# A hybrid encoder layer on one Trainium2 core: reordering the gate chain, delaying weight casts, pairing the gate projection, summing a chunk in PSUM

## Chip, core and metric

One NeuronCore of a Trainium2 chip runs the whole layer in one launch. The metric is the device time of that launch in microseconds (us); the kernel is timed in several runs, and the median is given. A further execution was recorded by the hardware profiler; its time stands beside its span below. Engines: TensorE (PE, with its weight loads PEld), VectorE (DVE), ScalarE (ACT), GpSimd (POOL), and SyncE (SP), which issues most DMAs.

## The reference, cut to what matters

An input x of 2048 positions x 1024 channels, float32, goes through one projection, two token mixers and an output projection:

```python
proj = einsum('bsd,de->bse', x, w_in[l])
q, k, v, gf_lr, gb_lr, z_gla, u, z_fnet = split(proj, _OFFSETS)
log_af = log_sigmoid(einsum(gf_lr, w_gate_up_fwd) + b_gate_fwd) / 16    # and log_ab for the other direction
o = gla_chunked(q * dk**-0.5, k, v, log_af) + flip(gla_chunked(flip(q), ..., flip(log_ab)))
o = o * rsqrt(mean(o * o, -1) + RMS_EPS)                                # per head
y_gla = o * gla_norm_g * silu(z_gla)
y_fnet = (real(fft2(u)) @ w_fnet) * silu(z_fnet)
y = concat([y_gla, y_fnet]) @ w_out
x = layernorm(alpha * x + y, ln_g, ln_b)
```

gla_chunked is gated linear attention (S_t = diag(a_t) S_{t-1} + k_t^T v_t, o_t = q_t S_t): inside a chunk, masked and decay-scaled scores times v; between chunks, a carried state S.

## The kernel before

Positions are cut into 8 blocks of 256 (`BLK`), each of two chunks of 128. Float32 operands are split into a high part in a reduced format (a ScalarE cast, line 55) and a low part (a VectorE subtraction, line 58); a product is three matmuls (high x high, high x low, low x high). `self.split` is the helper for both, so casts of x, of weights and of `mix` all carry lines 55 and 58. A scheduler of the language orders each engine's instructions at compile time, by the order of the source and by when it believes each to be ready. `tc.issue_after(ins)` adds an edge: every instruction in its block that runs on the engine of `ins` comes behind `ins` on that engine; instructions on other engines are not touched. Semaphores follow from the data.

PSUM has eight banks under three names: four `mm`, two `pa`, two `pg`.

*Phase 1* starts with the gate projection z_gla (`zg_first`, then `zg_block`). `zg_first` does blocks 0 and 1 while the weights arrive. `zg_block` does one block: for each of 4 column groups c, `proj_t` (line 86) runs 24 matmuls of 256 columns into one bank, and `zg_out` evicts it with Silu (262), scales it (263) and stores it (264). `load_x` brings the next block of x in two halves of 512 KB, a block ahead. A generator `bg` prepares the weights of the next stage in between. The other two projections, u and z_fnet, follow (line 349). `consts` casts the gate weights (466).

*Phase 2* is the Fourier mixer beside the q and k projections.

*Phase 3* (lines 898 to 953) loops over the blocks. For block b, in the order of the source: `pw_part` and `pv_part` (line 94) project v and the gate ranks; `gate_evac` and `gate_t` (755 to 788) turn the ranks (`rn`, `R`); `gates` (790) multiplies by the gate weights (798), applies Abs, Exp and Ln on ScalarE (800 to 803), finishes the log-sigmoid on VectorE (804) and runs two scans (809, 811): the first half of the gate chain. `gates2` (817), called an iteration later for the same block, is the second half: four small ScalarE copies (821 to 824), a VectorE subtraction and clip (825, 826), two ScalarE exponentials (828, 829), the scaling of q and k on VectorE (`scaled`, 845 and 846) and the decay factors (`alphas`). Then, for each chunk, `gla_a`: scores of both directions (855, 856), a transpose of the keys (859), the mask on VectorE (861, 862, tile `at`) and the eviction of the transposed keys on ScalarE (864, tile `ks`). `gla_b`: the state increment (874) from `ks`, evicted into S (876, 878), and the inner output (881) from `at`, evicted into `oi` (882). `gla_a` of a block's second chunk stands at the end of an iteration, its `gla_b` in the next. `chain_f` carries the forward state on GpSimd (`chain_step`, 1089 and 1092).

In iterations 2 to 5 `wof_load` brings half of the output weights: it loads two pieces of 256 KB (988) and splits them (989) in the same call. Behind the loop come `gates2` of block 7, `p4_start` (loads, `mix` heads and the other output weights), the first half of the output product of chunks 15 and 14 (`outp`, 1113) and the last two chunks' attention.

*Phase 4* goes over the chunks from 15 down. `prep(n)` carries the backward state (1149), multiplies q by the state (1153), adds `oi` (1155), squares (1157) and splits; `norm(n)` normalises, gates and splits into `mix`; `outp` adds the attention half to the output product; `finish` does the layer norm.

Each engine works through its own queue in order; SyncE's queue holds nearly all DMAs.

Of the kernel before, what the change touches and what calls it, by code (L numbers as in the profile page):

```python
# [19 lines left out]
P = 128  # L20
# [23 lines left out]
class Kern:  # L44
# [94 lines left out]
    def phase1(self):  # L139
# [3 lines left out]
        with ExitStack() as ctx:  # L143
# [116 lines left out]
            def zg_out(b, c, ps, zp):  # L260
                zs = zp.tile([P, BLK], F32, name="zs", tag=f"t{c}")
                nc.scalar.activation(out=zs, in_=ps, func=AF.Silu)
                nc.scalar.activation(out=zs, in_=zs, func=AF.Copy, scale=self.gn[:, c:c + 1])
                nc.sync.dma_start(out=self.zg_d[b][:, c], in_=zs)

            def zg_block(b, xh, bg, zp):
                for c in range(4):
                    ps = self.mm([P, BLK])
                    self.proj_t(ps, xh, self.wzg, c * P)
                    zg_out(b, c, ps, zp)  # L270
                    next(bg, None)

            with ExitStack() as rctx:
# [3 lines left out]
                xn = self.load_x(2)  # L277
# [4 lines left out]
                for b in range(2, NBLK - 1):  # L282
                    xh, xn = xn, self.load_x(b + 1)
                    zg_block(b, xh, bg, rp)
# [81 lines left out]
            def run(u, c, p, x):  # L366
# [56 lines left out]
            zg_block(NBLK - 1, xn, nxt, st)  # L423
# [28 lines left out]
    def consts(self):  # L452
# [13 lines left out]
        nc.scalar.copy(out=wg[0:97], in_=wgr)  # L466
# [258 lines left out]
    def phase3(self):  # L725
# [16 lines left out]
        with ExitStack() as ctx:  # L742
# [47 lines left out]
            def gates(b, blk):  # L790
                R = blk["R"]
                pool = gp if b % 2 else ga
                g = pool.tile([P, 4, BLK], F32, name="g", tag="g")
                for i in range(2):
# [6 lines left out]
                    with self.tc.issue_after(self.preload.ins):  # L801
                        nc.scalar.activation(out=gi, in_=gi, func=AF.Exp, scale=-1.0)
                    nc.scalar.activation(out=gi, in_=gi, func=AF.Ln, bias=one, scale=1.0)
# [40 lines left out]
            def scaled(blk):  # L844
                V.tensor_tensor(out=blk["q"], in0=blk["q"], in1=blk["eq"], op=ALU.mult)
                V.tensor_tensor(out=blk["ek"], in0=blk["kr"], in1=blk["ek"], op=ALU.mult)
                blk["k"] = blk["ek"]

            def gla_a(b, t, blk):
# [12 lines left out]
                V.copy_predicated(at.rearrange("p h i -> p (h i)"), mb, ab.rearrange("p h i -> p (h i)"))  # L862
                ks = gp.tile([P, 4, P], F32, name="ks", tag="ks", bufs=2)
                nc.scalar.copy(out=ks, in_=kt)  # L864
                blk["ak"].append((at, ks))

            def gla_b(b, t, blk):
# [12 lines left out]
                for h in range(4):  # L880
                    nc.tensor.matmul(op[:, h * P:(h + 1) * P], v[:, h * P:(h + 1) * P], at[:, h], start=True, stop=True)  # L881
                nc.scalar.copy(out=blk["oi"][:, t], in_=op)
# [14 lines left out]

            wof = self.wof_load()
            prev, old, xn = None, None, self.load_x(0)
            for b in range(NBLK):  # L900
# [9 lines left out]
                if b > 1:  # L910
                    gates2(b - 1, prev)
# [19 lines left out]
                if b == 1:  # L931
                    with self.tc.issue_after(R_ev.ins):
                        gates2(0, prev)
                elif b > 1:
# [18 lines left out]
            self.find_range(gp)  # L953

# [27 lines left out]
    def wof_load(self):  # L982
        nc = self.nc
        w = self.wof = self.wpool.tile([P, 2, 4, 1024], F32R, name="wB_w", tag="wB")
        for k in range(4):
            for c in range(0, 1024, 512):
# [289 lines left out]
```

## Time and profile before

| | us |
|---|---|
| median of 3 runs | 812.93 |
| lowest, highest | 809.15, 814.84 |
| profiled execution: its time | 808.7 |
| its span, first to last instruction | 806.8 |
| TensorE busy in the span | 758.7 |
| VectorE busy | 549.5 |
| ScalarE busy | 384.9 |
| GpSimd busy | 190.0 |

A busy time says how long an engine had an instruction running; it doesn't say whether the engine sets the time. That is read from its waits: for each instruction that started late, the profile names what released it.

### The profile page before, as it was taken

The page shows a single profiled execution, that of the slowest core. Times are in us where ns is not written, and L with a number is a line of the kernel's source. Part 1 is how long each engine was busy: PE and PEld are TensorE (multiplying, and loading weights), DVE is VectorE, ACT ScalarE, POOL GpSimd, SP SyncE. Part 2 cuts the span into 40 slices and gives each one's busy share as a digit, 9 for nine tenths or more (in the row PEclk, how much of TensorE's full clock was granted, in tenths as well). Part 3 has the DMA queues.
Part 4 walks back from the last instruction along what each step waited for, and adds up shares of the span by engine and source line. Part 5 has one row for each costly group of instructions (what it writes and reads, how often), then busy time and mean ns, then how long its engine had stood idle before and what let it go on. Part 6 is the DMA issues. An engine that isn't in the chain of part 4 may idle for free.

```text
span 806.8 us, 14100 instructions
## 1 busy us (share of the span) xinstructions
PE 758.7 (94%) x5542; PEld 713.7 (88%) x5542; DVE 549.5 (68%) x802; ACT 384.9 (48%) x730; POOL 190.0 (24%) x139
## 2 busy tenths in 40 slices
PE   7999999999999998999998898888798999999995
PEld 6999999999999998999997798887786788888884
DVE  4692197454535899776568887777667876776764
ACT  6684453322223534435346776756645344344341
POOL 0000003020201000321400421233234644644431
PEclk9999999999999999999999999998999999999998
DMA  8864434514136782647764655634247445435321
GB/s 253 255 223 157 149 110 143 165 66 144 66 113 185 242 284 89 191 143 223 229 183 157 184 175 191 183 107 132 76 137 281 146 159 189 157 138 178 107 89 70
DMA packets 76609, 130.52 MB, mean 162 GB/s; under 512 B 7315, under 2 KB 48787, under 8 KB 76534
## 3 DMA queue, kind: packets, MB, share of 16 engines
q1 hardware_dynamic: 74230, 125.34, 48.4%
q10 hardware_dynamic: 2304, 4.20, 1.5%
q8 instruction: 45, 0.74, 0.4%
q14 instruction: 30, 0.25, 0.1%
HBM read 92.81 MB, written 36.70 MB: 161 GB/s over the span
## 4 chain that ended last, share of the span: by engine, by line
PE 67%; DVE 17%; DMA 6%; ACT 5%; issue 3%; SPq 1%; POOL 0%; DVEq 0%; ACTq 0%; POOLq 0%
PE mm L1113 19%; PE mm L349 19%; PE mm L86 13%; PE mm L94 5%; DVE c L811 2%; DVE c L809 2%; PE pa L609 2%; DMA fw<-u_d 2%; PE pa L1153 2%; DVE g L825 1%; DVE fw L508 1%; PE pg L874 1%; DVE fw L505 1%; PE mm L231 1%; PE pg L881 1%
## 5 line engine op out<-in xcount | busy, mean ns | idle before, releaser
L94 PE MATMUL mm<-wA_w,xhl 128*128 128x272 f32 x768 | 106.2, 294 | 0.0
L94 PEld LDWEIGHTS mm<-wA_w,xhl 128*128 128x128 f32 x768 | 100.0, 192 | 0.0
L86 PE MATMUL mm<-xhl,wC_w 128*128 128x256 f32 x768 | 96.0, 284 | 0.0
L1113 PE MATMUL mm<-wA_w,mix 128*128 128x512 f32 (+1 forms) x396 | 92.7, 384 | 2.2 <-ACT mix L55 1.3
L86 PEld LDWEIGHTS mm<-xhl,wC_w 128*128 128x128 f32 x768 | 93.7, 192 | 0.5 <-issue 0.5
L1113 PE MATMUL mm<-wB_w,mix 128*128 128x512 f32 (+1 forms) x396 | 92.9, 390 | 0.0
L1113 PEld LDWEIGHTS mm<-wA_w,mix 128*128 128x128 f32 x396 | 72.6, 188 | 18.1 <-ACT mix L55 2.1
L1113 PEld LDWEIGHTS mm<-wB_w,mix 128*128 128x128 f32 x396 | 72.4, 190 | 13.7
L58 DVE TENSOR_TENSOR xhl<-xraw,xhl 128x1024 fp32r<-128x1024 f32 (+1 forms) x52 | 57.4, 1110 | 34.8 <-ACT xhl L55 33.7
L1089 POOL TENSOR_TENSOR S<-S 64x512 f32<-64x512 f32 x30 | 44.3, 1477 | 150.9 <-ACT S L876 147.3
L86 PE MATMUL mm<-xhl,wA_w 128*128 128x256 f32 x576 | 69.3, 283 | 0.0
L86 PEld LDWEIGHTS mm<-xhl,wA_w 128*128 128x128 f32 x576 | 69.2, 192 | 0.0
L55 ACT CAST xhl<-xraw 128x1024 fp32r<-128x1024 f32 (+1 forms) x52 | 49.2, 951 | 34.4 <-DMA xraw<-in_xt_dram 14.5
L58 DVE TENSOR_TENSOR x<-xraw,x 128x1024 fp32r<-128x1024 f32 x28 | 37.5, 1349 | 29.6 <-ACT x L55 29.6
L411 POOL TENSOR_TENSOR t<-t,t 128x512 f32<-128x512 f32 x7 | 11.0, 1580 | 191.4 <-ACT t L410 191.4
L1201 POOL TENSOR_TENSOR r<-r,lnb 128x1024 f32<-128x1024 f32 x15 | 36.1, 2408 | 80.8 <-issue 52.0
L55 ACT CAST x<-xraw 128x1024 fp32r<-128x1024 f32 x28 | 29.0, 1046 | 44.7 <-PE mm L349 37.8
L644 POOL TENSOR_TENSOR yf<-yf,zfl 128x256 f32<-128x256 f32 x24 | 21.1, 907 | 122.4 <-ACT yf L623 111.7
L349 PE MATMUL mm<-wC_s,x 128*128 128x256 f32 x384 | 48.3, 283 | 0.0
L349 PEld LDWEIGHTS mm<-wC_s,x 128*128 128x128 f32 x384 | 47.0, 192 | 0.1
L1092 POOL TENSOR_TENSOR S<-S,alpha 64x512 f32<-64x512 f32 x30 | 44.8, 1493 | 2.3
L874 PE MATMUL pg<-v,ks 128*128 128x128 f32 x128 | 19.6, 300 | 18.1 <-ACT ks L864 18.1
(193 smaller groups left out, 1451.3 us busy)
## 6 DMA issues: line engine op xcount, KB each, us to landing
xraw<-in_xt_dram SPq DMA_DIRECT2D x60, 512.0 KB, 5.0
xr<-in_x_dram SPq DMA_DIRECT2D x16, 512.0 KB, 3.8
out_dram<-r SPq DMA_DIRECT2D x15, 512.0 KB, 2.8
zg_d<-zs SPq DMA_DIRECT2D x32, 128.0 KB, 2.4
u_d<-t SPq DMA_DIRECT2D x16, 256.0 KB, 2.6
zf_d<-t SPq DMA_DIRECT2D x16, 256.0 KB, 2.5
zfl<-zf_d SPq DMA_DIRECT2D x32, 128.0 KB, 3.6
mf_d<-yf SPq DMA_DIRECT2D x16, 256.0 KB, 2.7
```

Source lines behind the costliest of these rows:

```text
L55: nc.scalar.copy(out=hi, in_=src)
L58: (lo_eng or nc.vector).tensor_tensor(out=lo, in0=src, in1=f32(hi), op=ALU.subtract)
L86: mm = self.nc.tensor.matmul(ps, w[:, s, k, c0:c0 + P], x[:, m, k % 4, :], start=(k == 0 and i == 0), stop=(k == KB - 1 and i == 2))
L94: self.nc.tensor.matmul(ps, x[:, s, k % 4, t * P:(t + 1) * P], w[:, m, k, c0:c0 + cols], start=(k == 0 and i == 0), stop=(k == KB - 1 and ...
L349: nc.tensor.matmul(ps[:, i], s_[s][:, k, i * P:(i + 1) * P], m_[m][:, k], start=(k == 0 and j == 0), stop=(k == 3 and j == 2))
L609: nc.tensor.matmul(yp[:, i], t[:, s, sl], et[:, mv, k1, off:off + 256], start=(j == 0), stop=(j == len(seq) - 1))
L644: (nc.gpsimd if g < 3 else nc.vector).tensor_tensor(out=yb, in0=yb, in1=zf, op=ALU.mult)
L874: nc.tensor.matmul(up[:, h * P:(h + 1) * P], ks[:, h], v[:, h * P:(h + 1) * P], start=True, stop=True)
L1089: E.tensor_tensor(out=S[ds, dst], in0=S[ds, dst], in1=S[ds, src], op=ALU.add)
L1092: E.tensor_tensor(out=d3, in0=d3, in1=al, op=ALU.mult)
L1113: nc.tensor.matmul(y, c["mix"][:, s, eb], w[:, v, eb % 4, lo:lo + m], start=(eb == 4 and i == 0), stop=(eb == 3 and i == 2))
L1201: nc.gpsimd.tensor_tensor(out=r, in0=r, in1=lnb, op=ALU.add)
```

## The change

1. `zg_block` becomes `zg_pair`: two blocks at once, matmuls of 512 columns into four banks, with x loaded in quarters of K for both blocks three steps ahead; `zg_out` evicts a pair.
2. `gates2` is pinned behind the last `ks` eviction (ScalarE) and the last mask (VectorE). `gates` is cut: Ln, log-sigmoid and scans become `gates1`, called behind `gla_a` of the previous block. In iteration 1 `gates2(0)` comes ahead of `gates(1)`, and `gates1(1)` is pinned behind the scaling of the keys.
3. `wof_load` splits a piece one iteration after its load, pinned behind the `oi` eviction and the key scaling; iterations 2 to 6.
4. Behind the loop `p4_start` is pinned behind `ks`; the output product of chunk 15 is interleaved with the attention, that of chunk 14 goes into phase 4, behind `prep(15)`. The inner output of chunk 15 stays in PSUM and the state part is added to it there (`fuse`). `find_range` comes ahead of the last `gla_b`.
5. The cast of the gate weights is pinned behind an eviction of phase 1 (`mid_ev`).

The diff, cut to its core:

```diff
-            def zg_block(b, xh, bg, zp):
-                for c in range(4):
-                    ps = self.mm([P, BLK])
-                    self.proj_t(ps, xh, self.wzg, c * P)
-                    zg_out(b, c, ps, zp)
-                    next(bg, None)
+            def zg_out(b, c, ps, zp, n=1):
+                zs = zp.tile([P, 2, BLK], F32, name="zs", tag=f"t{c}")
+                nc.scalar.activation(out=zs[:, 0:n], in_=ps, func=AF.Silu)
+                nc.scalar.activation(out=zs[:, 0:n], in_=zs[:, 0:n], func=AF.Copy, scale=self.gn[:, c:c + 1])
+                for i in range(n):
+                    nc.sync.dma_start(out=self.zg_d[b + i][:, c], in_=zs[:, i])
+            steps = [(pr, q) for pr in range(1, NBLK // 2) for q in range(4)]
+            def load_q(i):
...
+                raw = self.xpool.tile([P, 2, 2, BLK], F32, name="xraw", tag="xraw", bufs=2)
+                for b in range(2):
+                    nc.sync.dma_start(out=raw[:, :, b], in_=a["xt"][2 * pr + b, :, 2 * q:2 * q + 2, :])
+                t = self.xpool.tile([P, 2, 2, 2, BLK], F32R, name="xhl", tag="xhl", bufs=4)
+                self.split(t[:, 0], t[:, 1], raw)
...
+            def zg_pair(pr, bg, zp):
+                get = (self.mm,) * 4 if pr % 2 else (self.pa, self.pa, self.pg, self.pg)
+                ps = [g([P, 2, BLK]) for g in get]
+                for q in range(4):
+                    i = 4 * (pr - 1) + q
+                    load_q(i + 3)
+                    x = xq.pop(i)
+                    for c in range(4):
+                        for kk in range(2):
+                            for j, (s, m) in enumerate(((0, 0), (0, 1), (1, 0))):
+                                nc.tensor.matmul(ps[c], self.wzg[:, s, 2 * q + kk, c * P:(c + 1) * P], x[:, m, kk],
...
+                        if q == 3:
+                            zg_out(2 * pr, c, ps[c], zp, 2)
+                        if c % 2:
+                            next(bg, None)
...
-                xn = self.load_x(2)
+                for i in range(3):
+                    load_q(i)
...
+                for pr in (1, 2):
+                    zg_pair(pr, bg, rp)
...
-            zg_block(NBLK - 1, xn, nxt, st)
+            zg_pair(3, nxt, st)
...
-                    nc.scalar.copy(out=T(2), in_=ps)
+                    self.mid_ev = nc.scalar.copy(out=T(2), in_=ps)
...
+        with self.tc.issue_after(self.mid_ev.ins):
+            nc.scalar.copy(out=wg[0:97], in_=wgr)
...
+            def gates1(b, blk):
...
+                for z, gi in zs:
                     nc.scalar.activation(out=gi, in_=gi, func=AF.Ln, bias=one, scale=1.0)
...
                 if b > 1:
-                    gates2(b - 1, prev)
+                    with after(self.ks_ev, self.at_ev):
+                        gates2(b - 1, prev)
...
-                if 1 < b < 6:
-                    with self.tc.issue_after(self.x_dma.ins):
+                if 1 < b < 7:
+                    with after(self.x_dma, self.oi_ev, self.sc_ev):
                         next(wof)
...
+                if b == 1:
+                    with after(R_ev):
+                        gates2(0, prev)
                 gates(b, blk)
                 if b > 1:
                     gla_a(b - 1, 0, prev)
+                if b == 1:
+                    with after(self.sc_ev):
+                        gates1(b, blk)
+                else:
+                    gates1(b, blk)
...
             b = NBLK
-            gates2(b - 1, prev)
+            with after(self.ks_ev, self.at_ev):
+                gates2(b - 1, prev)
             gla_b(b - 2, 1, old)
             self.chain_f(2 * b - 3, 2 * b - 1)
-            self.p4_start(prev)
+            with after(self.ks_ev):
+                self.p4_start(prev)
             h15, h14 = self.head[NCH - 1], self.head[NCH - 2]
-            self.outp(h15, [4, 5, 6, 7])
+            self.outp(h15, [4, 5, 6, 7], (0,))
             gla_a(b - 1, 0, prev)
-            self.outp(h14, [4, 5, 6, 7], (0,))
+            self.outp(h15, [4, 5, 6, 7], (1,))
+            gla_a(b - 1, 1, prev)
             gla_b(b - 1, 0, prev)
             self.chain_f(2 * b - 1, 2 * b)
-            gla_a(b - 1, 1, prev)
-            gla_b(b - 1, 1, prev)
             self.find_range(gp)
+            gla_b(b - 1, 1, prev, True)
...
+        for k in range(5):
+            for raw, k0, c in todo:
+                self.split(w[:, 0, k0, c:c + 512], w[:, 1, k0, c:c + 512], raw)
+            todo = []
+            for c in (0, 512) if k < 4 else ():
                 raw = self.xpool.tile([P, 512], F32, name="wraw", tag="wraw", bufs=4)
                 nc.sync.dma_start(out=raw, in_=self.a["w_out"][:, 4 + k, c:c + 512])
+                todo.append((raw, k, c))
...
-                    nc.tensor.matmul(ip[:, hs], self.S[:, n, hs], qp[:, h], start=True, stop=True)
+                    nc.tensor.matmul(ip[:, hs], self.S[:, n, hs], qp[:, h], start=not fuse, stop=not fuse or h == 3)
+                if fuse:
+                    V.tensor_copy(out=o, in_=ip)
+                    nc.scalar.activation(out=sq, in_=ip, func=AF.Square)
...
             cur = prep(NCH - 1)
+            self.outp(self.head[NCH - 2], [4, 5, 6, 7])
             norm(cur)
-            self.outp(self.head[NCH - 2], [4, 5, 6, 7], (1,))
```

## Rows read from the trace of the kernel before

**Rows 1.** The page, part 1: engine, busy us (share of the span) x instructions

```profile
PE 758.7 (94%) x5542; PEld 713.7 (88%) x5542; DVE 549.5 (68%) x802; ACT 384.9 (48%) x730; POOL 190.0 (24%) x139
```

**Rows 2.** TensorE's waits, 402 to 640 us: us in total, times, longest

```profile
PE pg L874 <- ACT ks L864: 18.1, 12, 3.9
...
PE pa L855 <- DVE g L846: 2.8, 1, 2.8
...
PE pa L1153 <- POOL S L1092: 2.1, 3, 1.3
...
PE mm L1113 <- ACT mix L55: 1.3, 1, 1.3
```

**Rows 3.** Stretches: length; busy PE, PEld, DVE, ACT, POOL; granted clock; DMA share; GB/s

```profile
34.00:103.00 69.00, 69.00 (x577) 69.00 (x577) 32.37 (x39) 39.55 (x74) 0.00 (x0) 1.00 0.56 180
...
402.00:584.00 182.00, 159.25 (x1310) 151.52 (x1308) 138.62 (x172) 115.95 (x271) 44.49 (x28) 0.97 0.52 156
...
636.00:783.00 147.00, 147.00 (x697) 123.20 (x696) 103.52 (x144) 60.50 (x106) 71.01 (x45) 1.00 0.43 147
```

**Rows 4.** TensorE's timeline, two long waits: start, us, instruction, [idle before <-releaser]

```profile
487.77 1.16 PE L874 MATMUL pg<-v,ks 128*128 128x128 f32 x8 [2.68 <-ACT ks L864]
...
584.13 1.16 PE L874 MATMUL pg<-v,ks 128*128 128x128 f32 x8 [3.86 <-ACT ks L864]
```

**Rows 5.** The timeline of all engines from 487 us, one block

```profile
496.46 0.37 PE L855 MATMUL pa<-qp,g 64*128 64x128 f32 x1
...
502.80 2.29 DVE L811 TENSOR_TENSOR_SCAN c<-rst,g 64x1024 f32<-64x1024 uint8 x1
...
505.05 0.65 PE L859 MATMUL pg<-ident,g 128*128 128x128 f32 x4 [0.52 <-ACT S L878]
...
505.12 1.60 DVE L58 TENSOR_TENSOR wB_w<-wraw,wB_w 128x512 fp32r<-128x512 f32 x1
...
506.64 2.06 DVE L825 TENSOR_TENSOR g<-c 128x1024 f32<-128x1024 f32 x1
...
509.55 1.06 ACT L828 ACTIVATE c<-g 128x1024 f32<-128x1024 f32 x1 [2.52 <-DVE g L826]
...
510.35 0.73 DVE L862 COPY_PREDICATED at<-mb,pa 128x512 f32<-128x512 uint8 x1
...
510.51 0.57 ACT L864 COPY ks<-pg 128x512 f32<-128x512 f32 x1
...
511.13 1.16 PE L874 MATMUL pg<-v,ks 128*128 128x128 f32 x8 [2.42 <-ACT ks L864]
...
512.10 1.22 DVE L846 TENSOR_TENSOR g<-kr,g 128x1024 f32<-128x1024 f32 x1
```

**Rows 6.** Stretches behind the last three long waits

```profile
533.00:540.00 7.00, 6.28 (x39) 6.28 (x40) 3.01 (x4) 4.20 (x11) 2.31 (x2) 0.76 0.48 173
...
557.00:566.00 9.00, 7.23 (x36) 7.23 (x37) 4.60 (x9) 5.06 (x11) 2.30 (x2) 0.62 0.49 156
...
584.00:590.00 6.00, 5.86 (x26) 5.11 (x27) 5.94 (x9) 5.68 (x11) 2.86 (x2) 0.72 0.45 158
```

**Rows 7.** Stretch of one block, wait to wait

```profile
487.77:511.13 23.36, 20.27 (x174) 19.23 (x174) 18.99 (x24) 15.64 (x37) 5.32 (x4) 1.00 0.60 192
```

**Rows 8.** The chain that ended last: start, us, what

```profile
33.85 69.12 PE mm L86 x576
...
639.43 8.18 PE mm L1113 x36
```

**Rows 9.** DMA issues: line's tiles, count, KB each, median us to landing

```profile
raww<-in_xt_dram SPq DMA_DIRECT2D x4, 256.0 KB, 5.4
```

**Rows 10.** VectorE's timeline in the last block of the loop

```profile
577.67 3.18 DVE L811 TENSOR_TENSOR_SCAN c<-rst,g 64x1024 f32<-64x1024 uint8 x1
```

**Rows 11.** VectorE's timeline in the first blocks

```profile
435.03 1.23 DVE L846 TENSOR_TENSOR g<-kr,g 128x1024 f32<-128x1024 f32 x1
```

**Rows 12.** GpSimd's timeline in the last block of the loop

```profile
578.77 2.90 POOL L1092 TENSOR_TENSOR S<-S,alpha 64x512 f32<-64x512 f32 x1
```

More of the change, by code (lines that the diff above doesn't have):

```diff
@@ new lines, in phase1 @@
+            steps = [(pr, q) for pr in range(1, NBLK // 2) for q in range(4)]
+            xq = {}
+            def load_q(i):
+                if i >= len(steps):
+                    return
+                pr, q = steps[i]
+                raw = self.xpool.tile([P, 2, 2, BLK], F32, name="xraw", tag="xraw", bufs=2)
[3 more added lines that the diff above has]
+                self.split(t[:, 0], t[:, 1], raw)
+                xq[i] = t
@@ new lines, in zg_pair @@
+            def zg_pair(pr, bg, zp):
[9 more added lines that the diff above has]
+                                nc.tensor.matmul(ps[c], self.wzg[:, s, 2 * q + kk, c * P:(c + 1) * P], x[:, m, kk],
+                                                 start=(q == 0 and kk == 0 and j == 0), stop=(q == 3 and kk == 1 and j == 2))
+                        if q == 3:
+                            zg_out(2 * pr, c, ps[c], zp, 2)
+                        if c % 2:
+                            next(bg, None)
@@ L793, in gates @@
                 g = pool.tile([P, 4, BLK], F32, name="g", tag="g")
+                zs = []
                 for i in range(2):
@@ L861, in gla_a, with gla_b @@
                 V.tensor_tensor(out=at, in0=af, in1=mf.rearrange("p (o i) -> p o i", o=1).broadcast_to([P, 4, P]), op=ALU.mult)
-                V.copy_predicated(at.rearrange("p h i -> p (h i)"), mb, ab.rearrange("p h i -> p (h i)"))
+                self.at_ev = V.copy_predicated(at.rearrange("p h i -> p (h i)"), mb, ab.rearrange("p h i -> p (h i)"))
                 ks = gp.tile([P, 4, P], F32, name="ks", tag="ks", bufs=2)
-                nc.scalar.copy(out=ks, in_=kt)
+                self.ks_ev = nc.scalar.copy(out=ks, in_=kt)
                 blk["ak"].append((at, ks))
-            def gla_b(b, t, blk):
+            def gla_b(b, t, blk, fuse=False):
                 n = 2 * b + t
@@ L880, in gla_b @@
                 for h in range(4):
-                    nc.tensor.matmul(op[:, h * P:(h + 1) * P], v[:, h * P:(h + 1) * P], at[:, h], start=True, stop=True)
-                nc.scalar.copy(out=blk["oi"][:, t], in_=op)
+                    nc.tensor.matmul(op[:, h * P:(h + 1) * P], v[:, h * P:(h + 1) * P], at[:, h], start=not fuse or h == 0, stop=not fuse)
+                if fuse:
+                    blk["op"] = op
+                    return
+                self.oi_ev = nc.scalar.copy(out=blk["oi"][:, t], in_=op)
                 if t == 1 and b < NBLK - 1:
@@ L896, in alphas, with after @@
                 nc.scalar.activation(out=alpha[64:128, lo + 1:n1 + 1], in_=tf[64:128, 0:m], func=AF.Exp, scale=1.0 / TAU)
+            def after(*evs):
+                es = ExitStack()
+                for e in evs:
+                    es.enter_context(self.tc.issue_after(e.ins))
+                return es
             wof = self.wof_load()
@@ L929, in phase3 @@
                     gla_a(b - 1, 0, prev)
+                if b == 1:
[3 more added lines that the diff above has]
+                    gates1(b, blk)
                 pv = pv_part(xh, 1, blk, None, range(5))
[L931 to L934, printed above, removed]
+                if b > 1:
                     gla_b(b - 1, 0, prev)
@@ L1202, in finish @@
                 nc.sync.dma_start(out=a["out"][n * P:(n + 1) * P, :], in_=r)
-            h15 = 1
-            for h in self.head.values():
-                if "y" not in h:
-                    self.outp(h, [4, 5, 6, 7], (0, 1)[:h15 + 1])
-                h15 = 0
+            if "y" not in self.head[NCH - 1]:
+                self.outp(self.head[NCH - 1], [4, 5, 6, 7])
             cur = prep(NCH - 1)
+            self.outp(self.head[NCH - 2], [4, 5, 6, 7])
             norm(cur)
-            self.outp(self.head[NCH - 2], [4, 5, 6, 7], (1,))
             for n in range(NCH - 1, -1, -1):
```

35 lines of the change are left out of this document (17 added, 18 removed).

## The prediction

> **What bounds the kernel now.** I read the page first, then TensorE's waits, then the span by stage, and only then single blocks. The page says that TensorE is busy for 94% of the span and no other engine for more than 68% [rows 1]; so time can come off in two ways: by filling TensorE's idle stretches, or by giving it less or faster work. In the waits the reader should see where the idle time sits: 18.1 us of it are waits of line 874 for the eviction `ks` on ScalarE, 2.8 us one wait for the keys of line 846 on VectorE, 2.1 us are three waits for the state chain at the start of phase 4, 1.3 us one for a cast there [rows 2]. The stages say the same: 34 to 103 us, the gate projection, is full, and so is phase 4 from 636 us; phase 3, 402 to 584 us, has 159.3 us of work in 182.0 and a mean clock of 0.97 [rows 3]. In a full stage only less work helps.
>
> Of the 12 waits in the 18.1 us six are over 2 us, one in each iteration of phase 3 from the third on (2.68 us in one of the full blocks) and one behind the loop (3.86 us). They sum to 16.5 us, and the six others to 1.6 us [rows 2, 4]. The order of one block shows why [rows 5]. VectorE ends its second scan at 505.1 us, casts an output weight, and runs line 825 of `gates2`. On ScalarE the exponential of line 828 waits for that half of the chain until 509.55 us. The copy `ks` is queued behind it and starts at 510.51 us; its transposes on TensorE were done at 505.7 us. TensorE, which had nothing more from 508.7 us, goes on at 511.13 us. So a copy of 0.57 us waits for a gate chain that nobody needs before line 855 of the next block.
>
> The clock rides on these waits. After the last three of them TensorE's granted clock stood at its lower level, 1.2 instead of 2.4 GHz, for about 3.4, 6.8 and 3.4 us: the means of three stretches are 0.76 of 7 us, 0.62 of 9 and 0.72 of 6 [rows 6]. Their missing parts are 1.7, 3.4 and 1.7 us; less 0.4 us that fell into a wait, 6.4 us were lost. The wait before 487.77 us, of 2.68, was followed by a block at 1.00 [rows 4, 7].
>
> **The change part by part.** The sum is made against the profiled execution: a span of 806.8 us, with 1.9 us around it 808.7. The median of the runs shown is 812.93, 4.2 more; I carry that difference over.
>
> *Gate projection in pairs.* 576 matmuls of 256 columns become 288 of 512. The 576 take 69.12 us, 120.0 ns each; the output projection's matmuls of 512 columns run 36 in 8.18 us, 227.2 ns each [rows 8]. 288 x (2 x 120.0 - 227.2) = 3.7 us less, and as TensorE is full there, it comes off the span. 24 evictions of two ScalarE instructions become 12 longer ones: worth nothing, because ScalarE isn't the bound. The loads become 24 DMAs of 256 KB instead of 12 of 512 KB on SyncE's queue, some behind the eight stores at a pair's end. A load of that size landed in 5.4 us [rows 9]; it is issued three steps of 24 matmuls ahead, 16.4 us, which hides it, a cast and a subtraction of 1 to 1.2 us each and some us of queue. If this cover failed, each step would wait; I take 0, with the whole 3.7 us as the other end. The Trainium skill (TensorE: Matmul & The Clock Gate, Back-to-back issue gap) gives isolated warm matmuls N/2.4 + 2.5 ns; by that a pair saves one 2.5 ns, an estimate of 0.7 us in all. The rows differ by 12.8 ns a pair, and the measurement decides.
>
> *Eviction and mask ahead of `gates2`.* A pin orders only instructions of one engine: ScalarE's exponentials come behind `ks`, VectorE's line 825 behind the masked scores of line 862. The six long waits, 16.5 us, go. What is late next? `ks` is then ready about 0.7 us after its transposes, before TensorE comes to it. The masked scores follow the scan: 505.1 + 1.4 = 506.5 us, wanted 1 us after line 874 starts, at 509.7. The keys: from line 825's start to line 846's end it is 6.7 us (506.64 to 513.32) [rows 5], so 513.2 us again, and line 855, at 496.46 us in this block, would come at about 517.5 in the next if a block takes 21 us: 4 us of slack. Behind them on VectorE stand line 757, on which the next gate hangs, and the splits of x; they start no later than before, since a cast leaves their way. In the block after the loop the cover is thinner. Its scan ends at 580.85 us [rows 10], the mask at 582.3, and TensorE, free at 580.3 (584.13 - 3.86), would want it for line 881 at 581.2: 1.1 us of wait. Its keys come at 582.3 + 6.2 = 588.5; 19 of chunk 15's 24 output matmuls are left to fill (4.3 us, to 587.7): 0.8 us more, or 3.5 if half of them stand behind line 855. I charge 1.9 us (ends 0 and 4.6). The casts of `p4_start`, pinned behind `ks` there too, have time until phase 4.
>
> *The first blocks.* `gates2(0)` stands ahead of `gates(1)`, and the latter's scans behind the key scaling. Before, line 846 came after both scans of `gates(1)`, at 435.0 us [rows 11]; now the keys come ahead of them, at least 4.6 us earlier (two scans of 2.29), and the wait of 2.8 us for them goes. The pin of the gate weights' cast (line 466) moves it inside phase 1, where TensorE is full and nobody wants it: 0.
>
> *Weight casts a block later.* ScalarE's waits for these DMAs go; it isn't the bound, so 0. The subtraction of 1.60 us [rows 5] leaves the way between scan and line 825. It comes back behind the key scaling, where VectorE waited for ScalarE's cast of the gate ranks; if that cover is gone, the next gate's transposes wait up to 1 us in four blocks.
>
> *Slack that isn't there.* A block of 23.36 us holds 20.27 us of TensorE and 18.99 us of VectorE [rows 7]. Without its long wait it is 20.9 us long, and VectorE's loop, 19.0 us and about 0.9 for the exponential that it must wait for, needs 19.9. That is close; I charge 0.3 us for each of six blocks, 1.8 us (ends 0 and the first rival's 6.6 more).
>
> *Clock.* With the waits ahead of them the slow stretches go: 6.4 us (ends 0 and 6.4, since the rows show only that one follows the other).
>
> *Chunk 15.* Its inner part stays in PSUM: ScalarE's copy of it goes, the addition becomes a copy, and the square reads PSUM beside it. The 24 output matmuls of chunk 14 come to stand in its normalisation, where TensorE waited 2.1 and 1.3 us [rows 2]. They are 5.4 us of filling for 3.4 us of waits; but 2.7 us of them filled there already, and the chain is serial. I take half, 1.7 us (ends 0 and 3.4). `find_range` ahead of the last `gla_b` is a few short instructions: 0.
>
> Sum: 3.7 + 16.5 - 1.9 + 2.8 - 1.8 + 6.4 + 1.7 = 27.4 us: 781.3 for a profile like this one, 812.9 - 27.4 = 785.5 for the median.
>
> **Rivals.** (A) VectorE becomes the bound of phase 3. For it: the second scan took 2.29 us in one block [rows 5] and 3.18 in another [rows 10], where a GpSimd product of 2.90 us ran beside it [rows 12]; shorter blocks put the same GpSimd work beside more of VectorE's. With the long scan, and two waits left in the block (0.9 for the cast of x, 0.6 for the scores), the loop is 19.9 + 0.9 + 1.5 = 22.3 us, 1.1 more than my 21.2; in six blocks 6.6 us: 792.1. Against it: a late VectorE shortens both waits. By the Trainium skill (SBUF — State Buffer, Who interferes with whom) a VectorE instruction with two SBUF inputs and a GpSimd one that reads SBUF exclude each other; the two scans agree, which speaks against this change.
>
> (B) The clock falls anyway, after shorter waits or those behind the loop, and 6.4 us stay: 791.9. For it: not every long wait was followed by the lower level, so length alone doesn't set it.
>
> (C) The change doesn't do what it says: the waits of phase 3 keep their sum, since another instruction takes the exponential's place ahead of `ks`, and only the pairs remain: 812.9 - 3.7 = 809.2. Against it: the rows show one culprit in ScalarE's queue.
>
> (D) Slower: the wait moves to line 855. Line 825 may now not start before the masked scores, which need TensorE's scores at the end of a block; if the weight casts (2.3 us), line 757 (0.4) and the splits of x (2.4, with a wait for ScalarE) stand ahead of the key scaling as well, the keys come 6 us later, at 519 instead of 513.2, or later still. With a wait w in six blocks, and the lower clock after each of seven waits at the mean of the three (2.1 us, so 15.0 instead of 6.4), it decides where 6w + 8.6 = 16.5 + 2.8 + 3.7, at w = 2.4 us. At w = 4 it costs 9.6 us: 822.5. Against it: the 4 us of slack.
>
> **How the numbers follow.** Forecast 0.58, A 0.16, B 0.10, C 0.08, D 0.08. The first three, and a little of C, are faster by over 1% (about what a measurement of this kernel can tell from no change): 0.86. The rest of C lies within 1%: 0.07. D is slower: 0.07. The range goes from 776, where none of the charges falls due, chunk 15's filling is complete (785.5 - 1.9 - 1.8 - 1.7 = 780.1) and the runs spread as shown (5.7 us, so some 4 below a median), to 800, which holds A and B together (798.5).
>
> **What would show it.** Right: line 874's waits for `ks` under 4 us in all; blocks of about 21 us; a granted clock of 1.00 in the whole of phase 3; 288 matmuls of 128x512 in some 65.5 us. Line 855 waiting for line 846, or line 787 for line 757, in each block would show D or A. Wrong in the sum: gaps at the steps of the pairs, or keys of the last block later than the output matmuls reach.

## The result, and the profile after

The changed kernel takes 803.78 us (median of 7 runs, 801.42 to 804.15), the kernel before 812.93 (809.15 to 815.05): a ratio of 0.9891, interval 0.9863 to 0.9918, 1.1% faster. The forecast was 785.5, its range 776 to 800. So the sign was right, and two thirds of the gain never came. The profile of before is a run of 808.7 us, 4.2 below its median, so the two profiles lie 4.8 us apart where the medians lie 9.15.

Line numbers move: the lines 757, 787, 825, 828, 846, 855, 862, 864, 874, 881 and 1113 of before are 783, 813, 859, 862, 880, 889, 896, 898, 908, 915 and 1168 now.

The page of the changed kernel, its span and part 1, to be held against [rows 1]:

```profile
span 802.0 us, 13525 instructions
...
PE 754.5 (94%) x5254; PEld 698.1 (87%) x5254; DVE 545.2 (68%) x802; ACT 382.4 (48%) x705; POOL 199.4 (25%) x139
```

TensorE's idle time is the span less its busy time: 806.8 - 758.7 = 48.1 us before, 802.0 - 754.5 = 47.5 us now. It is busy for 4.2 us less, but next to nothing of its waiting is gone. Where it waits now, in the stretch of [rows 2]:

```profile
PE mm L813 <- DVE rn L783: 12.5, 6, 3.1
PE pg L915 <- DVE rn L783: 3.2, 1, 3.2
PE mm L1168 <- DVE mix L58: 2.6, 3, 1.6
PE pg L915 <- DVE at L896: 1.8, 1, 1.8
...
PE pg L908 <- ACT ks L898: 1.6, 2, 0.9
PE pa L889 <- DVE g L880: 1.1, 2, 0.6
```

Line 908's waits for `ks` fell from 18.1 to 1.6 us, as forecast. In their place line 813, the transposes of the gate ranks, waits 12.5 us for line 783: 3.15, 2.93, 2.96 and 2.37 us in the four iterations that cast weights, 0.84 in the one behind them. The second row is one wait, at 434.64 us; line 915 reads the mask's tile `at`, so what it waited for is the mask, which ended just ahead of the instruction named. The timeline of one block shows why line 813 waits:

```profile
509.95 4.76 PE L94 MATMUL mm<-wA_w,xhl 128*128 128x272 f32 x36
...
510.69 1.06 ACT L862 ACTIVATE c<-g 128x1024 f32<-128x1024 f32 x1 [2.51 <-DVE g L860]
...
514.20 0.59 ACT L919 COPY oi<-pg 128x512 f32<-128x512 f32 x1
...
515.14 1.14 ACT L55 CAST wB_w<-wraw 128x512 fp32r<-128x512 f32 x2
...
515.79 1.83 DVE L58 TENSOR_TENSOR wB_w<-wraw,wB_w 128x512 fp32r<-128x512 f32 x2 [1.55 <-ACT wB_w L55]
516.18 0.18 ACT L781 CAST rn<-mm 128x32 fp32r<-128x32 f32 x1
...
517.55 0.18 DVE L783 TENSOR_TENSOR rn<-mm,rn 128x32 fp32r<-128x32 f32 x1
...
517.78 0.45 PE L813 MATMUL mm<-ident,rn 128*96 128x128 f32 x1 [2.96 <-DVE rn L783]
```

The 36 matmuls end at 514.7 us; the last 12 of them belong to the next projection, so the ranks' own matmuls were done at about 513.1. But ScalarE, which must cast them, first runs the exponentials (released at 510.69), the evictions queued behind these, and then the weight casts, which the change pinned behind the `oi` eviction of line 919: exactly ahead of the rank cast. VectorE repeats it: two weight subtractions, 1.83 us, ahead of the 0.18 us that TensorE waits for. The clock, in stretches behind the four waits (columns as in [rows 3]):

```profile
468.00:476.00 8.00, 6.58 (x48) 6.33 (x49) 5.62 (x9) 5.98 (x12) 0.11 (x1) 0.79 0.86 239
492.00:500.00 8.00, 6.34 (x47) 6.09 (x48) 5.76 (x9) 6.02 (x14) 0.35 (x1) 0.79 0.85 246
516.00:524.00 8.00, 6.22 (x35) 5.77 (x36) 4.51 (x7) 5.93 (x13) 0.47 (x1) 0.57 0.85 236
541.00:546.00 5.00, 3.28 (x33) 3.11 (x33) 4.29 (x6) 4.30 (x11) 0.41 (x1) 1.00 0.83 211
```

Missing are 8 x (0.21 + 0.21 + 0.43) = 6.8 us, what [rows 6] had lacked. A fourth fall comes on top, behind the wait at 434.64 us: the clock's mean is 0.79 from 434 to 442 us, 1.7 us more. The pairs came as written; the chain has their 288 matmuls (96, then 8 x 12, then 96) from 34.67 to 99.98 us, 65.3 us in place of 69.12 [rows 8]:

```profile
34.67 21.79 PE mm L291 x96
56.46 2.72 PE pa L291 x12
...
78.22 21.76 PE mm L291 x96
```

### The profile page after: what moved, and what is told of

Read it like the earlier page. It is cut to its first block, busy times and chain, and to the rows that moved or that the text cites. A ratio compares the mean times of both kernels' runs of the same rounds, so it can differ in the third digit from the quotient of the medians.

```text
span 802.0 us, 13525 instructions
## 1 busy us (share of the span) xinstructions
PE 754.5 (94%) x5254; PEld 698.1 (87%) x5254; DVE 545.2 (68%) x802; ACT 382.4 (48%) x705; POOL 199.4 (25%) x139
## 4 chain that ended last, share of the span: by engine, by line
PE 62%; DVE 17%; ACT 9%; DMA 6%; issue 3%; POOL 2%; SPq 1%; DVEq 0%; ACTq 0%; POOLq 0%
PE mm L374 19%; PE mm L1168 19%; PE mm L291 5%; PE mm L86 4%; PE mm L94 3%; DVE c L845 3%; DVE c L843 2%; DVE fw L534 2%; DMA fw<-u_d 2%; PE pa L635 2%; PE pa L1214 1%; DVE fw L531 1%; PE pg L291 1%; PE pa L291 1%; PE mm L231 1%
## 5 line engine op out<-in xcount | busy, mean ns | idle before, releaser
L94 PE MATMUL mm<-wA_w,xhl 128*128 128x272 f32 x768 | 110.1, 300 | 0.0
L94 PEld LDWEIGHTS mm<-wA_w,xhl 128*128 128x128 f32 x768 | 103.2, 197 | 0.0
L1144 POOL TENSOR_TENSOR S<-S 64x512 f32<-64x512 f32 x30 | 51.5, 1718 | 137.2 <-ACT S L910 135.4
L58 DVE TENSOR_TENSOR xhl<-xraw,xhl 128x1024 fp32r<-128x1024 f32 (+1 forms) x52 | 58.0, 1118 | 27.2 <-ACT xhl L55 27.0
L670 POOL TENSOR_TENSOR yf<-yf,zfl 128x256 f32<-128x256 f32 x24 | 21.5, 923 | 119.5 <-ACT yf L649 110.8
L1147 POOL TENSOR_TENSOR S<-S,alpha 64x512 f32<-64x512 f32 x30 | 47.4, 1580 | 2.7 <-ACT alpha L932 0.4
L291 PE MATMUL mm<-xhl,wA_w 128*128 128x512 f32 x192 | 43.9, 389 | 0.0
L291 PEld LDWEIGHTS mm<-xhl,wA_w 128*128 128x128 f32 x192 | 36.0, 188 | 7.4
L55 ACT CAST mix<-zg 128x512 fp32r<-128x512 f32 x16 | 9.9, 622 | 57.2 <-POOL zg L1235 55.9
```

Source lines behind the costliest of these rows:

```text
L55: nc.scalar.copy(out=hi, in_=src)
L58: (lo_eng or nc.vector).tensor_tensor(out=lo, in0=src, in1=f32(hi), op=ALU.subtract)
L94: self.nc.tensor.matmul(ps, x[:, s, k % 4, t * P:(t + 1) * P], w[:, m, k, c0:c0 + cols], start=(k == 0 and i == 0), stop=(k == KB - 1 and ...
L291: nc.tensor.matmul(ps[c], self.wzg[:, s, 2 * q + kk, c * P:(c + 1) * P], x[:, m, kk], start=(q == 0 and kk == 0 and j == 0), stop=(q == 3 ...
L670: (nc.gpsimd if g < 3 else nc.vector).tensor_tensor(out=yb, in0=yb, in1=zf, op=ALU.mult)
L1144: E.tensor_tensor(out=S[ds, dst], in0=S[ds, dst], in1=S[ds, src], op=ALU.add)
```

## The experiments

Each ratio is against runs of the kernel before on the same chip. Over the sets of runs the median of before lies between 810.4 and 812.9 us, so a difference between kernels of two sets is good to about 2 us.

**The weight casts.** Theory: their new place costs the waits of line 813. Rival: these waits belong to the delayed gate chain, wherever the casts stand. Three kernels move nothing but the casts and the issue of their loads. The first puts them behind the cast `R` of the transposed ranks:

```diff
-                    with after(self.x_dma, self.oi_ev, self.sc_ev):
+                R_ev = gate_t(blk)
+                    with after(self.x_dma, R_ev, self.rn_lo):
                         next(wof)
```

> The changed kernel with one thing moved: in each block the two weight casts and their subtractions stand behind the gate ranks (ScalarE: behind the cast of R, line 814; VectorE: behind line 783) and no longer ahead of them. Theory 1, the delayed weight casts hold up the gate ranks: the waits of line 813 for line 783 (12.5 us in six, four of them in blocks with casts at 2.4 to 3.2) fall to that of the block without casts, 0.84 each, so 12.5 becomes about 4.5; the lower clock behind three of these waits, 6.8 us, goes; 803.8 - 8 - 6.8 = 789, between 785 and 794. Theory 2, the ranks are late because `gates2` and the evictions now stand ahead of them on both engines, casts or not: the waits stay above 2 us each, and the time stays within 800 to 805.

796.34 us, ratio 0.9808 (0.9748 to 0.9869): between the two theories' times. The second restores the casts of before, in the load's own iteration and without the pins:

> The changed kernel with the weight casts as in the kernel before: loaded and split in the same call, blocks 2 to 5, pinned only on SyncE. Theory 1: the ranks wait under 1.2 us per block, but ScalarE holds `ks` behind a cast that waits for its DMA, so line 908 waits for `ks` instead, 1 to 3 us in four blocks, with the lower clock behind some of them: 795 to 803. Theory 2: line 813's waits stay above 2 us and the others come on top: 805 to 812.

797.22 us, ratio 0.9821 (0.9758 to 0.9884): theory 1 by its time, but what line 915 waits for, 1.4 us in the blocks with casts, is the mask, behind 1.95 us of weight subtractions on VectorE, and not `ks`. The third puts them where ScalarE has a pause, behind the last small copy of `gates2`, and their subtractions behind line 783:

```diff
-                    with after(self.x_dma, self.oi_ev, self.sc_ev):
+                    with after(self.x_dma, self.cst_ev, self.rn_lo):
```

> The changed kernel with one thing other: the two weight casts of an iteration stand on ScalarE behind the last small copy of gates2 (line 858), where ScalarE waits for VectorE's clip, and their subtractions on VectorE behind that of the ranks (line 783). All other instructions of both engines keep their order. Theory 1 (the loop of ScalarE's and VectorE's stretches sets the block; the casts cost because they lengthen it): blocks of 24.1 to 24.9 us become 20.9 to 21.3, granted clock 1.00 in them, time 789 to 792. Theory 2 (VectorE's own work sets the block, so its casts cost wherever they stand): blocks of 22.0 us or more, 795 to 798.

794.29 us, ratio 0.9799 (0.9761 to 0.9838): 9.5 us less (7.5 by the ratios) for one displaced pair of casts. The time lies between the two theories', the blocks are nearer to the first. One block from transposes to transposes, in each of the three and in the changed kernel; first the changed kernel:

```profile
493.66:517.78 24.12, 21.16 (x174) 20.38 (x174) 18.79 (x24) 15.93 (x37) 8.40 (x4) 0.92 0.50 154
```

casts_behind_R:

```profile
487.59:509.66 22.07, 20.41 (x175) 19.19 (x176) 18.25 (x23) 15.85 (x37) 8.59 (x5) 1.00 0.54 167
```

idle_casts_alone:

```profile
491.17:512.62 21.45, 20.13 (x174) 19.12 (x174) 18.88 (x24) 16.04 (x37) 8.37 (x5) 1.00 0.57 172
```

In casts_as_before the blocks with casts are 23.3 us long, those without 21.45. Against 21.45 the same casts cost 2.7 us a block in the changed kernel's place (with the fall of the clock), 1.9 in that of before, 0.6 behind R and nothing in the pause: what counts is what stands behind them. The rival falls for two thirds of the wait; 0.8 to 1.05 us of it stay in all three.

**The parts alone.** On the kernel before, only the pins of `gates2` and `gates1` and that of the gate weights' cast; then only the pairs; then casts_behind_R without the pairs.

> The kernel before with the second half of the gate chain pinned and cut as in the change, and nothing else of it (weight casts, pairs, end and phase 4 as before; the inner output of chunk 15 is not fused). Theory 1: as casts_as_before plus the 3.7 us of the pairs and about 2 us of the end: 800 to 808, the waits of line 874's successor for `ks` 1 to 3 us in the four blocks with casts and under 0.5 elsewhere. Theory 2: the wait for line 783's predecessor at the gate transposes, above 2 us in each block: 809 to 815.

802.78 us, ratio 0.989 (0.9828 to 0.9951): theory 1 by its time, by other waits than it named (below).

> The kernel before with the gate projection in pairs alone. Both theories: 3.7 us less than before (288 matmuls at 227 ns for 576 at 120), 809.2 where before is at 812.9; phase 3 unchanged in its waits. If pairing hides or costs something at its borders, 812 or more.

810.82 us, ratio 0.999 (0.9959 to 1.0022): no gain that can be told.

> As casts_behind_R, but the gate projection as before, one block at a time with matmuls of 256 columns. Theory 1 (pairs are worth their 3.7 us; in pairs_only clock falls in phase 3 hid them): 3.7 us more than casts_behind_R, 799.5 to 800.5, and the stage of the gate projection 69.1 instead of 65.3 us. Theory 2 (the pairs' gain is given back by later stages, as the ratio 0.999 of pairs_only suggests): 796 to 797.5.

799.63 us, ratio 0.9847 (0.9813 to 0.9881): 3.3 us more than casts_behind_R, and its 576 matmuls take 69.12 us again. So with the rest of the change the pairs are worth 3.3 us between medians, and 69.12 - 65.31 = 3.8 in their stage. In pairs_only something hid them. Its profile shows it in the stage behind: without part 5 of the change the cast of the gate weights (line 491 there) waits for its DMA at the head of ScalarE's queue, for 10.48 us. The evictions come behind it, TensorE waits for one of them, and its clock falls:

```profile
120.97 0.62 ACT L491 CAST wg<-wgr 97x512 fp32r<-97x512 f32 x1 [10.48 <-DMA wgr<-in_wg_dram]
...
125.58 4.63 PE L374 MATMUL mm<-wB_s,x 128*128 128x256 f32 x24 [1.94 <-DVE t L428]
```

```profile
125.00:131.00 6.00, 5.42 (x32) 5.42 (x33) 5.90 (x6) 1.06 (x1) 4.18 (x2) 0.72 0.45 118
```

The wait and 6 x 0.28 us of clock are 3.6 us, the whole gain: from the first matmul of the pairs to the one that starts at 225.09 us it is 189.9 us, as long as in before (190.3); the changed kernel, with the cast pinned, needs 186.3 for the same work. Before has the unpinned cast too, waiting 8.59 us, but no wait of TensorE behind it. No run takes the pin alone out of the changed kernel.

This profile is also the slowest of ten runs, 814.5 us long. It has the long waits for `ks`, and the clock fell behind more of them: it is 0.57, 0.72 and 0.72 in three stretches of 12 us from 436, 488 and 564 us, 11.9 us missing. Why more often in this run stays open. It isn't what hid the pairs in the median: over the ten runs the mean clock was 0.971 to 0.984, over the 13 runs of before 0.973 to 0.985.

The pins alone give 811.25 - 802.78 = 8.5 us where the sum had 22.0 (16.5 + 2.8 + 6.4 - 1.9 - 1.8). Their profile tells why; TensorE's timeline of one block of gate_pins_only, and its length (lines 871, 758, 789, 890, 788 and 800 there are 896, 783, 814, 915, 813 and 825 of the changed kernel):

```profile
493.92 0.74 PE L800 MATMUL mm<-R,wg 98*128 98x256 f32 x4 [0.50 <-ACT R L789]
...
508.12 1.13 PE L890 MATMUL pg<-at,v 128*128 128x128 f32 x8 [1.40 <-DVE at L871]
...
514.93 0.32 PE L788 MATMUL mm<-ident,rn 128*96 128x128 f32 x1 [1.04 <-DVE rn L758]
```

```profile
491.61:514.93 23.32, 20.38 (x174) 19.21 (x175) 18.94 (x23) 15.96 (x37) 8.36 (x5) 1.00 0.64 204
```

A block of before took 23.36 us [rows 7]. The wait of 2.4 us for `ks` became three, 1.40 for the mask, 1.04 for the ranks, 0.50 for `R`: within a block with casts at full clock the pins gain nothing. They gain in the blocks behind: 21.45 and 23.19 us, at a clock of 1.00, where before took 22.59 and 25.05, the latter at 0.92. Behind the loop some is lost again, by a wait of 4.51 us for the mask (1.1 were charged) and a fall of the clock: 0.76 of 14 us from 572 on.

**The clock.** Does a fall cost time, or does it lie beside a chain that sets the block anyway? 12 extra matmuls, whose result is overwritten, ahead of the rank transposes in four blocks of the changed kernel:

```diff
+                if 2 < b < 7:
+                    for k in range(4):
+                        for j in range(3):
+                            nc.tensor.matmul(pv, xh[0][:, 0, k, 0:P], wvg[:, 0, k, 0:272], start=True, stop=True)
```

> The changed kernel, with 12 more matmuls of 272 columns (their result is overwritten) ahead of the rank transposes in the four blocks with weight casts: 1.4 us of extra work put into waits of about 3 us. Theory 1 (TensorE's clock falls behind waits of that length, and the falls cost time): waits of line 813 of about 1.6 us, granted clock 1.00 in these blocks, and the 6.8 us missing behind the waits at 469, 493 and 517 us come back: 796.5 to 798.5 where the changed kernel had 803.8. Theory 2 (the clock falls whatever the wait's length, or the falls lie beside a chain that sets the block anyway): 803 to 806.

799.54 us, ratio 0.9848 (0.9807 to 0.989). One of the stretches, at a clock of 1.00 as the other three are:

```profile
487.00:495.00 8.00, 6.54 (x59) 6.03 (x58) 6.62 (x9) 7.29 (x16) 0.98 (x1) 1.00 0.86 251
```

and the wait that is left in it, from TensorE's timeline:

```profile
489.29 0.31 PE L813 MATMUL mm<-ident,rn 128*96 128x128 f32 x1 [1.46 <-DVE rn L783]
```

48 matmuls more, some 5.4 us of work (12 of them take 1.36), and 4.2 us less time. No fall is left in phase 3 of this profile, a run of 794.7 us. Three blocks take 22.9 us each, with the extra work, where the changed kernel's took 24.2, 24.1 and 24.9. The profiled run is the fastest of five, but all five have a mean clock of 0.990 to 0.996, the changed kernel's seven 0.979 to 0.986. So the falls did cost, and theory 1 holds in kind; the median stayed 1 us above its range.

**What sets a block of 22 us.** First two changes to casts_behind_R. The exponentials behind the rank cast:

```diff
+                with after(self.rn_ev):
                     nc.scalar.activation(out=eq, in_=g, func=AF.Exp, scale=1.0 / TAU)
```

> As casts_behind_R, with the two exponentials of gates2 (lines 862 and 863) pinned behind the cast of the second half's gate ranks on ScalarE. Theory 1 (ScalarE's queue: the rank casts came 2 us after their matmuls because the exponentials and the evictions released by them stood ahead): the six waits of line 813 (5.4 us) go, except the latency of cast, subtraction and transpose; blocks of 22.07 us become 21.0 to 21.4; time 791 to 793.5 where casts_behind_R had 796.3. Theory 2 (the chain rank, gate, scan, mask, exponential, keys sets the block): the wait only changes its place, to line 889 for the keys or line 825 for R; time 795 to 799.

799.91 us, ratio 0.9853 (0.9811 to 0.9895). Theory 2, a little above its time: the wait of line 813 is gone, but line 890, the scores, now waits 6.1 us in all, in six places, for the keys, and the mask's reader 5.6 in four; blocks are 23.3 us. Next, the steps of `chain_f` on GpSimd held until the second scan has ended:

> As casts_behind_R, with the steps of chain_f on GpSimd held until the block's second scan has ended (a GpSimd copy of one of its elements goes ahead of them). Theory 1 (rival A: VectorE sets the block, and its second scan takes 3.20 instead of 2.29 us because GpSimd's product of 2.91 us runs beside it): second scans of 2.3 us, GpSimd products of 1.0 to 1.4 us, blocks of 22.07 us become 21.1 to 21.4, time 791 to 793.5 where casts_behind_R had 796.3. Theory 2 (ScalarE's queue and the chain of the ranks set the block): the scans get shorter too, but blocks stay at 21.8 to 22.1 us and the time at 795 to 797.

795.41 us, ratio 0.9808 (0.9757 to 0.9859): no gain, theory 2. casts_behind_R had this in its timeline:

```profile
497.95 3.20 DVE L845 TENSOR_TENSOR_SCAN c<-rst,g 64x1024 f32<-64x1024 uint8 x1
...
499.07 2.91 POOL L1147 TENSOR_TENSOR S<-S,alpha 64x512 f32<-64x512 f32 x1
```

and chain_after_scan this:

```profile
499.94 2.29 DVE L845 TENSOR_TENSOR_SCAN c<-rst,g 64x1024 f32<-64x1024 uint8 x1
...
503.91 1.90 POOL L1151 TENSOR_TENSOR S<-S,alpha 64x512 f32<-64x512 f32 x1
...
504.84 1.00 DVE L929 TENSOR_TENSOR cend<-cend,cmid 128x8 f32<-128x8 f32 x1
...
505.76 0.15 DVE L929 TENSOR_TENSOR cst<-cst,cmid 128x8 f32<-128x8 f32 x1
```

The scan lost its 0.9 us, and a subtraction of 8 elements, 0.15 us otherwise, took 1.00 and ended with GpSimd's product: the cost moved past three instructions to the fourth, and the block stayed at 22.1. The chain that ended last in casts_behind_R says what the block is made of:

```profile
487.33 1.05 ACT xhl L55
...
488.64 0.95 ACT xhl L55
...
489.85 1.04 ACT wB_w L55 x2
...
491.17 0.98 ACT g L827 x2
492.15 1.04 ACT g L829 x2
...
495.65 2.28 DVE c L843
...
497.95 3.20 DVE c L845
...
502.71 1.10 DVE g L859
...
504.66 1.06 ACT c L862
```

TensorE has no long piece on it: the loop runs through ScalarE (exponentials, evictions, rank casts, casts of x and of weights, the gate) and then VectorE (scans, mask, clip). From the rank cast at 487.03 us to the next at 509.10 the chain is 12.4 us on ScalarE and 9.7 on VectorE, together the block of 22.07. Either engine has pauses, but in turn. Next, on chain_and_first (described below), half of ScalarE's casts of x behind R:

> As chain_and_first, with the cast of the second half of the next x on ScalarE behind the cast R of line 814. Theory 1 (R waits in ScalarE's queue behind both casts of x): the five waits of line 825 (2.2 us) go, blocks 0.4 to 0.6 us shorter, 2 to 3 us less than chain_and_first. Theory 2 (VectorE sets the block, and its subtraction of x now comes later): no difference within 1 us, or up to 2 us more.

793.56 us, ratio 0.977 (0.9725 to 0.9814), 3.3 more than chain_and_first: theory 2, and worse than it gave; line 813 waits longer for what line 825 no longer does. Other ways to shorten ScalarE's stretch: in the changed kernel the weight casts on GpSimd, and on idle_casts (below) the casts of x in the pause too.

> The changed kernel with the output weights' casts of wof_load on GpSimd, both parts, without the pin behind eviction and key scaling. Theory 1 (it is the casts' 1.15 us on ScalarE and 2.3 us on VectorE ahead of the rank casts that cost): all blocks from the third on at 20.8 to 21.5 us, no wait of line 813 over 1.2 us, time 789 to 793. Theory 2 (GpSimd's work beside VectorE's scans costs as much): scans of 3.2 us instead of 2.3 and the carried state late, time 796 to 803.

799.45 us, ratio 0.9842 (0.9796 to 0.9888): the last two blocks with casts take 24.1 (with a fall of the clock) and 23.2 us, the two without 21.5. Theory 2, but not by the scans, whose second takes 2.54 and 2.29 us in these blocks: line 859 took 1.96 and 2.51 us instead of 1.21 beside GpSimd's work.

> As idle_casts, with both casts of the next x on ScalarE in that pause too, and their subtractions on VectorE behind that of the ranks. Theory 1: ScalarE's stretch is another 2.1 us shorter; TensorE with its 20.1 us of work then sets the block: 20.2 to 20.6 us, 782 to 785. Theory 2 (the casts of x don't fit into the pause beside the weight casts, so they delay the exponentials and with them the keys): a wait of line 889 of 1 us or more in each block, 787 or more.

792.8 us, ratio 0.978 (0.9741 to 0.9819). Theory 2 by its time, but not by its wait for the keys: x took the pause, and the displaced weight casts stood ahead of the rank cast again (waits of line 813 up to 2.2 us). With them behind R instead (on chain_and_first):

> As chain_and_first, with both casts of the next x on ScalarE behind the last small copy of gates2, in its pause ahead of the exponentials; the weight casts stay behind R. Theory 1 (the loop of ScalarE's and VectorE's stretches sets the block): 2.1 us less in ScalarE's stretch, of which TensorE's 20.1 to 20.4 us of work let 1.5 us show: blocks of 20.4 to 20.8 us instead of 22.1, time 783 to 785.5 where chain_and_first had 790.2. Theory 2 (the rest of the loop gives it back, by late keys or by VectorE): blocks of 21.5 us or more, 788 or more.

790.77 us, ratio 0.975 (0.9686 to 0.9813), as chain_and_first: theory 2. Its chain:

```profile
507.07 3.01 DVE xhl L58 x2
510.08 1.20 DVE wB_w L58 x2
...
513.23 1.18 DVE g L838 x2
...
514.50 2.28 DVE c L843
...
516.80 2.29 DVE c L845
...
520.67 1.11 DVE g L861
521.79 0.92 DVE cend L929
...
523.50 1.06 ACT c L864
```

Now it is VectorE nearly all the way round, with the exponentials; blocks of 22 us again. Once ScalarE's part is shortened, VectorE takes over: rival A's end state.

**The first blocks, and the fastest version.** On chain_after_scan, the scans of `gates1(1)` also behind the mask of block 0:

```diff
-                    with after(self.sc_ev):
-                        gates1(b, blk)
...
+                if b == 1:
+                    with after(self.sc_ev, self.at_ev):
+                        gates1(b, blk)
```

> As chain_after_scan, and in iteration 1 the scans of gates1(1) come behind the mask of block 0's first chunk instead of between its two halves. Theory 1 (the wait of 3.2 us at 434 us is for that mask, behind two scans): this wait goes, and with it the clock's fall behind it: 3 to 5 us less than chain_after_scan. Theory 2 (the time is taken back by block 1's keys, which come later): a wait of 2 us or more for keys or ranks in iteration 2, and no more than 1 us less.

790.24 us, ratio 0.9737 (0.9689 to 0.9785): 5.2 us less than chain_after_scan, with the wait at 434 us gone, so theory 1. The same with the casts in the pause:

> As chain_and_first, with the weight casts as in idle_casts_alone instead of behind R. Theory 1: 1.1 us less in each of four blocks, 785 to 787 where chain_and_first had 790.2. Theory 2: blocks stay at 22.1 us, 789.5 to 791.

789.67 us, ratio 0.9751 (0.9714 to 0.9789); blocks with casts are 21.5 us instead of 22.1, so 0.6 us less and not the 1.1 of theory 1, and the time, theory 2's, is the same within its spread. Both are some 14 us below the changed kernel by the medians, 11 to 13 by the ratios.

## Why the prediction was wrong

Taken in this order the differences of the medians are: pins 8.5 (forecast 22.0), pairs 3.3 (3.7), the end with chunk 15 2.3 (1.7), weight casts 797.22 - 803.78 = -6.6 (0). They make up the 9.15 us but for the 1.7 between the two medians of before, by construction and not as a check: the end is what is left of the 5.6 us between gate_pins_only and casts_as_before, and the pins were measured with the casts in the place of before. What came back says more. Of the 18.3 us by which the forecast was missed, 9.5 came back with the weight casts in ScalarE's pause, and 5.2 with the scans of the first blocks behind the mask. idle_casts, which has both, is 4.2 us above the forecast.

- *Pairs:* 3.8 in the stage where 3.7 were worked out; 3.3 between medians. They leaned on the pin of the gate weights' cast, which the prediction priced at 0 because "nobody wants it": without it the next stage took 3.6 us back.
- *Long waits for `ks`:* gone, as said. But 16.5 us of waits were counted as gained; in a block with casts none of it was. The step that failed is "they start no later than before, since a cast leaves their way". It followed line 757 on VectorE alone. Its input comes from ScalarE, where the exponentials, the evictions and the delayed weight casts now stand ahead of the rank cast: line 813 waits 2.4 to 3.2 us in four blocks, and 0.8 to 1.05 in the three kernels that move the casts.
- *Weight casts:* the same step, seen from ScalarE: "it isn't the bound, so 0", with "up to 1 us in four blocks" as the end. They cost 6.6 us against their place of before and 9.5 against the pause: the delay put them ahead of the rank cast, on both engines. The prediction saw the place and priced it by VectorE's own pause; the casts came later than that pause.
- *Slack:* 0.3 us a block for the closeness of TensorE and VectorE. TensorE's 20.9 us and VectorE's 19.9 were compared, but the loop uses ScalarE and VectorE in turn: 21.45 to 22.1 us once the casts are moved, against 21.2. Without weight casts in the way the forecast of 21.2 was close.
- *Clock:* the falls behind the old waits went, and others came behind line 813's and behind the wait at 434 us: 6.8 us missing before, 8.5 after. Rival B's outcome, by other waits.
- *First blocks:* the wait of 2.8 us for the keys went (0.56 left), but the scans, put behind the key scaling, stood between the mask's two halves: 3.2 us, and a fall of the clock in this profile. Behind the mask they cost 5.2 us less.
- *Behind the loop:* 1.9 us were charged, 1.1 for the mask and 0.8 for keys. The mask's wait is 1.8 us; the keys' is 0.5, but line 1168 waits 1.6 for the low part of `mix`, whose casts, pinned behind `ks`, start at 576.87 us. The prediction gave these casts "time until phase 4"; chunk 15's output product reads them ahead of it.
- *Chunk 15:* the 2.1 us of waits for the state chain are gone; those for casts of `mix` in the normalisation are 1.41, 0.55, 0.20 and 0.52 us, where 1.28 and 0.85 stood. That is 1.5 us of the 1.7.
- *Rivals:* in the changed kernel as a whole C came closest (TensorE's waits from 402 to 640 us were 27.2 us and are 25.8), though its culprit was another. D's wait at line 889 stayed at 0.6 us. A described what is left once the casts are moved.

## What to carry to other kernels

A pin doesn't only hold an instruction back; it chooses what stands behind it. Before pinning, name the next instruction on that engine that another engine waits for, and follow its inputs on every engine. Where two engines work in turn, add their stretches round the loop; comparing each engine's sum hides the bound. And price a wait together with the clock behind it: here 5.4 us of throw-away work in four waits took 4.2 us off the time. A part that pays nothing alone may need another part: the pairs paid nothing in the run without a pin that had been priced at 0.

## What the runs showed of the hardware

GpSimd and VectorE paid for each other in these rows: a scan took 3.20 instead of 2.29 us beside a product, 8 elements 1.00 instead of 0.15, and the product itself 2.91 where it took 1.03 alone (at 434.88 us in the changed kernel); held back from the scan, it hit a later instruction. The Trainium skill (SBUF — State Buffer, Who interferes with whom), weighed in the prediction, says that a VectorE instruction with two SBUF inputs and a GpSimd one that reads SBUF exclude each other; these rows agree.

A wait's length alone doesn't tell whether the clock falls to 1.2 GHz: behind the wait at 434 us, 3.2 us long in both, it fell in the changed kernel (0.79 from 434 to 442) and not in the profiled run of casts_behind_R (1.00); behind 2.37 us at 542.72 it didn't, behind 2.96 at 517.78 it did, and in exps_behind_ranks it fell behind 1.25 us at 538.67 (0.80 from 538 to 542). Putting work into the wait kept it at 1.00 in refill's profile.
